# Keeping the low halves of split weights in DRAM between the two segments of a hybrid decoder block

## The chip, the cores and the metric

The kernel runs on one core of one Trainium2 chip. The metric is device time in microseconds. A core has TensorE (PE: matmuls, with PEld for its weight loads), VectorE (DVE), ScalarE (ACT), GpSimd (POOL) and SyncE (SP, which here only issues DMAs). Each engine works through its own instruction queue in order; DMAs are issued from the queues of SyncE, ScalarE or GpSimd and are moved by 16 DMA engines.

## The reference

The block takes 1024 tokens of width 1024, puts 16 meta tokens ahead of them, and applies a half-step SwiGLU, a mixer, a second half-step SwiGLU and a final norm, all in float32:

```python
h = h + 0.5 * _swiglu(_rmsnorm(h, ffn1_norm[l]), ffn1_w_gu[l], ffn1_w_down[l])
u = _rmsnorm(h, mix_norm[l])
aq, ak, av, az, abeta, aalpha, bcols, ga, gb = jnp.split(u @ w_in[l], ...)
o_a = _deltanet_branch(...)      # chunked gated DeltaNet, 8 heads of 128
o_b = _rwkv7_branch(...)         # RWKV-7 time mixing, 16 heads of 64
merged = jax.nn.sigmoid(ga) * o_a + jax.nn.sigmoid(gb) * o_b
h = h + merged @ w_out[l]
h = h + 0.5 * _swiglu(_rmsnorm(h, ffn2_norm[l]), ffn2_w_gu[l], ffn2_w_down[l])
```

The change touches the product `u @ w_in` alone, and of that only how its weights come to the chip.

## The kernel before

**Precision.** TensorE multiplies numbers of a shortened float32 format (F32R). To keep float32 accuracy each operand is split into a high part, the value rounded to F32R, and a low part, the rest. `split` (L159) does this with two instructions: ScalarE copies the source into the high part (L163), and VectorE subtracts that from the source for the low part (L164). `mm3` (L309) then adds three products for each of the eight slices of 128 rows: high weight with high data, high weight with low data, low weight with high data. So the low half of a weight tile is first wanted by the third product.

**Weights.** `w_in` is stored as 75 tiles `in_win[ct]` of 128 x 8 x 128 (512 KB each, 4 KB in a partition). `fetchw` (L251) loads one of them with a DMA of SyncE (L268) into a raw buffer `wraw` (two of these), then splits it into a buffer `w` of shape [128, 2, 8, 128] (two, `WB`): index 0 of the second axis is the high half, 1 the low half. `loadw` (L279) is called when a projection begins; it fetches up to one tile ahead of the one in use (`AHEAD`), so the tile after the current one is written into the buffer that the previous projection has just left.

**Two segments.** The 1040 columns of the mixer (16 meta tokens and 1024 tokens) are done in two segments: the first has the meta tokens and 512 tokens, the second the other 512. In each segment the 8 head groups j are gone through, so there are 16 steps, `it` = 0 to 15, and each weight tile is loaded and split twice, once in each segment. `USES` (L168) names the tiles of a step: 48+j, 40+j, 32+j in `new_b` (value, key and receptance of the RWKV part), 8+j, j, 16+j in `new_a` (key, query and value of the DeltaNet part) and 24+j, 59+j, 67+j in `gates`. Tiles 56 to 58 belong to `segment`, which works once for each segment. In the first segment a projection of `new_b` and `new_a` has 528 columns, in two parts; in the second all have 512, with 24 matmuls.

**Order.** The actions of a step are listed by hand in strings such as

```python
REGULAR = "merge_blocks transitions operands+ inverses+ chains gates finish decay++ new_b++ new_a++"
```

where a `+` means one step ahead, so several steps are in flight. The framework traces the program in this order and then plans the order of each engine's queue itself; it also puts in all waits. So instructions of several actions stand mixed in one queue. In one step of the second segment, `chains` runs the recurrences over chunks while projections fill the gaps (products p, pq, b); `inverses` is a long row of small VectorE instructions (tb at L1657, Xb at L1659) ending in a copy (Yt, L1660) that goes out by DMA; `new_b` turns the three projections into rB, kB, kkn, AR, BK and bv, and `bon` is a product of the split of bv; `merge_blocks` and `transitions` make products xp, vp, mp and np, with ScalarE copies (xa, at, xv) between.

**GpSimd's queue in the mixers** has small work: zeroing the first columns of `sh` and `xr`, saving the last columns of a segment (carB, carA), the memsets of the inverses (Xb), copies of XA, egl, gam, and the start state SBs of the chain. DMAs from its queue occur once before the mixers' steps (rdr) and around the output projection (h2dr, h3dr); ScalarE's queue issues DMAs only at the kernel's beginning and end.

Of the kernel before, what the change touches and what calls it, by code (L numbers as in the profile page):

```python
# [8 lines left out]
F32 = mybir.dt.float32  # L9
F32R = mybir.dt.float32r  # L10
AF = mybir.ActivationFunctionType
ALU = mybir.AluOpType

P = 128
D = 1024
KD = D // P
# [21 lines left out]
NJ = 8  # L38
# [72 lines left out]
def build(tc, nc, a):  # L111

    ctx = ExitStack()
    with ctx:
        g = K()
        g.tc, g.nc, g.a = tc, nc, a
        nc.scalar.preload_act_table_set("natural_log_exp_and_others")
        pad = ctx.enter_context(tc.tile_pool(name="pad", bufs=1, side="right"))
        nc.vector.memset(pad.tile([P, 24], F32, name="pad"), 0.0)
        const = ctx.enter_context(tc.tile_pool(name="const", bufs=1))  # L120
        wp = ctx.enter_context(tc.tile_pool(name="wp", bufs=2))
        dram = ctx.enter_context(tc.tile_pool(name="dram", bufs=1, space=bass.MemoryType.DRAM))
        g.mmctx = ctx.enter_context(ExitStack())
        main_banks(g, 2, 3, 8)
        g.const, g.wp, g.dram = const, wp, dram

        ones = const.tile([P, P], F32, name="ones")
        nc.vector.memset(ones, 1.0)
        g.pk = const.tile([P, NPK], F32, name="pk")
        nc.sync.dma_start(g.pk, a["pk"])  # L130

        def pv(n):
            o, w = PK[n]
            return g.pk[:, o : o + w]

        nc.vector.tensor_scalar(pv("omu"), pv("mu"), -1.0, 1.0, op0=ALU.mult, op1=ALU.add)
        nc.vector.tensor_scalar(pv("oka"), pv("ka"), -1.0, 1.0, op0=ALU.mult, op1=ALU.add)
        for n in ("w0", "a0"):
            nc.vector.tensor_scalar(pv(n), pv(n), -1.0, None, op0=ALU.mult)
        g.C = lambda n: ones if n == "ones" else g.ck[:, CK[n][0] - P : CK[n][0] - P + CK[n][1]]  # L140
        g.V = lambda n, i=0: g.pk[:, PK[n][0] + i : PK[n][0] + i + 1]

        hdr = [dram.tile([KD, P, sn], F32, name=f"hdr{s}") for s, (_, sn, _) in enumerate(SEGS)]
        mdr = [dram.tile([NJ, P, FULL], F32, name=f"mdr{s}") for s in range(2)]
        g.hdr, g.mdr = hdr, mdr
        g.sdr = dram.tile([NJ, P, P + CB], F32, name="sdr")
        g.gdr = [dram.tile([NJ, FULL], F32, name=f"gdr{s}") for s in range(2)]
        g.rdr = dram.tile([P, FULL], F32, name="rdr")
        g.h2dr = dram.tile([KD, P, FULL], F32, name="h2dr")
        g.h3dr = dram.tile([KD, P, FULL], F32, name="h3dr")  # L150
        g.frm = dram.tile([len(FORMS), HF, P, T // 2], F32, name="frm")

        g.worder, g.wready, g.wfetched, g.wused = list(weight_order()), [], 0, 0
        ffn1(g)
        middle(g)
        ffn2(g)


def split(g, src, hi, lo, eng=None, hi_eng=None):  # L159
    if hi_eng:  # L160
        hi_eng.tensor_copy(hi, src)
    else:
        g.nc.scalar.activation(hi, src, AF.Copy)  # L163
    (eng or g.nc.vector).tensor_tensor(lo, src, hi.bitcast(F32), op=ALU.subtract)  # L164


LORA = (56, 57, 58)
USES = {"segment": LORA, "new_b": (48, 40, 32), "new_a": (8, 0, 16), "gates": (24, 59, 67)}  # L168


def schedule():

    last = 2 * NJ - 1
    yield "segment", 0
    for act in FIRST.split():
        yield act.rstrip("+"), act.count("+")
    for it in range(last + 1):
        order = {NJ - 2: BEFORE_SWITCH, NJ - 1: SWITCH, last - 1: LAST_BUT_ONE, last: FINAL}.get(it, REGULAR)
        for act in order.split():
            if act == "segment":  # L180
                yield act, 1
            else:
                yield act.rstrip("+"), it + act.count("+")
# [11 lines left out]
def weight_order():  # L195

    def down_order(n):
        for r in range(len(FORMS)):
            for m in range(HK):
                for k0, kk in CHUNKS:  # L200
                    yield f"wdn{n}", (r, m, k0), kk

    def tiles(cts, j=0):
        for ct in cts:
            yield "win", (ct + j % NJ,), KD

    yield from down_order(1)
    for act, it in schedule():
        yield from tiles(USES.get(act, ()), 0 if act == "segment" else it)
    for _ in range(2):  # L210
        for m in range(KD):
            yield "wout", (m,), KD

    yield None
    yield from down_order(2)
# [14 lines left out]
def down_weights(g, name, raw, r, m, k0, kk, copied):  # L230

    s = g.wsum[:, m, k0 : k0 + kk]
    if r == 4 and k0 == 0:
        in_turn(g, g.wsum[:, m], block(g, name, m, 0, 0))
    if raw is None:
        return s
    i, j = ((1, 0), (0, 0), (0, 1), None, (1, 0), (0, 1))[r - 1]
    in_turn(g, raw, g.wlast[m, :, k0 : k0 + kk] if copied else block(g, name, m, i, j, k0, kk))
    if r == LAST:
        return raw  # L240
    x, y = (raw, s) if r == 3 else (s, raw)
    g.nc.gpsimd.tensor_tensor(s, x, y, op=ALU.add if r == 1 else ALU.subtract)  # L242
    return s


def held(g, what):

    return what[0].startswith("wdn") and what[1][0] == LAST and len(g.held) > 0


def fetchw(g):  # L251
    if not g.worder[g.wfetched]:
        del g.worder[g.wfetched]
    name, idx, kk = g.worder[g.wfetched]
    g.wfetched += 1
    down = name.startswith("wdn")
    raw = w = None
    if held(g, g.worder[g.wfetched - 1]):
        w = g.held.pop(0)
        raw = w[:, 1, :kk].bitcast(F32)  # L260
    elif not down or idx[0] not in (0, 4):
        raw = g.wp.tile([P, KD, P], F32, name="wraw", tag="wraw", bufs=2)[:, :kk]
    if down:
        src = down_weights(g, name, raw, *idx, kk, w is not None)
        g.wcount += 1
    else:
        src = raw
        g.nc.sync.dma_start(raw, g.a[name][idx])  # L268
    if w is not None:
        pass  # L270
    elif down and g.wcount % 3 == 0:
        w = g.wthird.tile([P, 2, CHUNKS[0][1], P], F32R, name="w3", tag="w3", bufs=1)
    else:
        w = g.wp.tile([P, 2, KD, P], F32R, name="w", tag="w", bufs=WB)
    split(g, src, w[:, 0, :kk, :], w[:, 1, :kk, :])
    g.wready.append((name, idx, w))


def loadw(g, name, *idx):  # L279

    while g.wfetched < len(g.worder) and g.worder[g.wfetched]:
        down = g.worder[g.wfetched][0].startswith("wdn")
        if g.wfetched > g.wused + AHEAD + down and not held(g, g.worder[g.wfetched]) or (name == "wdn1" and not down):
            break
        fetchw(g)
    g.wused += 1
    n, i, w = g.wready.pop(0)
    assert (n, i) == (name, idx)
    return w


def main_banks(g, w, n, banks=6):

    g.mmctx.close()
    g.mmw = w
    pool = lambda name, bufs: g.mmctx.enter_context(
        g.tc.tile_pool(name=name, bufs=bufs, space=bass.MemoryType.PSUM, reuse_waits="tile"))
    g.mm = pool("mm", n)
    g.mx = pool("mx", banks - n * w)
# [356 lines left out]
class Hidden:  # L656
# [16 lines left out]
    def ahead(self):  # L673
        g = self.g
        g.wcount, g.turn, g.held, g.direct = 0, None, [], self.direct
        sums = lambda m: g.nc.sync.dma_start(g.wsum[:, m], block(g, self.name, m, 1, 1))
        self.even += self.places("11", "21")
        self.slots = self.even[:]
        self.load(8, 0)
        yield  # L680
        yield
        sums(0)
        fetchw(g)
        self.split(3)
        yield
        self.even += self.places("t2")
        self.slots = self.even[:HF]
        self.load(HF, 0)
        self.split(6)
        yield  # L690
        sums(1)
        self.split(8)
        yield
        fetchw(g)
        self.split(HF - 1)
        for m in (2, 3):
            sums(m)
        yield
# [1296 lines left out]
```

## Time and profile before

| what | value |
|---|---|
| median of 3 runs | 2974.12 us (2969.96 to 2985.99) |
| profiled execution | 2974.08 us, span 2972.3 us |
| busy share, PE / DVE / ACT / POOL | 97% / 74% / 49% / 17% |
| L164 low parts from `wraw`, whole kernel | 254, 338.2 us |
| L163 high parts from `wraw`, whole kernel | 254, 266.9 us |
| `wraw<-in_win` | 150 DMAs of 512 KB, SyncE's queue |
| GpSimd's DMA queue | 2000 packets, 6.56 MB |
| ScalarE's DMA queue | 2016 packets, 2.63 MB |

The two SwiGLUs take the time up to about 700 us and from about 2300 us on; the mixers lie between, their first segment up to about 1480 us. In the page's list of instruction groups one line such as L164 gathers every use of `split`, with its mean over different shapes, so times of one use are better read from the row of a single instruction. A row of the timeline gives start, length, engine, line, operation and tiles, and in brackets how long the engine stood idle before it and what released it.

### The profile page before, as it was taken

The page shows a single profiled execution, that of the slowest core. Times are in us where ns is not written, and L with a number is a line of the kernel's source. Part 1 is how long each engine was busy: PE and PEld are TensorE (multiplying, and loading weights), DVE is VectorE, ACT ScalarE, POOL GpSimd, SP SyncE. Part 2 cuts the span into 40 slices and gives each one's busy share as a digit, 9 for nine tenths or more (in the row PEclk, how much of TensorE's full clock was granted, in tenths as well). Part 3 has the DMA queues.
Part 4 walks back from the last instruction along what each step waited for, and adds up shares of the span by engine and source line. Part 5 has one row for each costly group of instructions (what it writes and reads, how often), then busy time and mean ns, then how long its engine had stood idle before and what let it go on. Part 6 is the DMA issues. An engine that isn't in the chain of part 4 may idle for free.

```text
span 2972.3 us, 63124 instructions
## 1 busy us (share of the span) xinstructions
PE 2876.8 (97%) x25720; PEld 2496.4 (84%) x25720; DVE 2208.8 (74%) x4121; ACT 1450.5 (49%) x2559; POOL 503.4 (17%) x578
## 2 busy tenths in 40 slices
PE   8999999999899999999998999999999999999998
PEld 8999999999878888888776777777777888888887
DVE  8666668776667877788878887778876766667886
ACT  6322234346555656565566556556644422223443
POOL 0332232323000000000000000001101032332431
PEclk9999999999999999999999999999999999999999
DMA  5333236553232322333232332333345332333763
GB/s 212 125 108 108 98 124 206 182 193 118 71 70 72 86 65 68 84 81 85 89 98 73 80 79 77 76 87 82 106 132 185 127 109 99 97 102 130 248 220 113
DMA packets 287907, 339.39 MB, mean 114 GB/s; under 512 B 172704, under 2 KB 181024, under 8 KB 287616
## 3 DMA queue, kind: packets, MB, share of 16 engines
q1 hardware_dynamic: 283600, 326.17, 36.0%
q0 software_dynamic: 2000, 6.56, 0.6%
q8 instruction: 202, 3.31, 0.5%
q10 hardware_dynamic: 2016, 2.63, 0.2%
q14 instruction: 89, 0.73, 0.1%
HBM read 267.63 MB, written 73.41 MB: 115 GB/s over the span
## 4 chain that ended last, share of the span: by engine, by line
PE 67%; DVE 19%; ACT 6%; issue 3%; DMA 3%; SPq 1%; POOL 0%; DVEq 0%; ACTq 0%; POOLq 0%
PE pg L521 25%; PE pp L315 15%; PE pd L742 10%; DVE w L164 3%; PE pwo L315 2%; PE pg L545 2%; DVE tb L1657 1%; DVE Xb L1659 1%; DVE form L164 1%; ACT w L163 1%; PE vp L1342 1%; DMA form<-frm 1%; PE mp L1342 1%; PE xp L1342 1%; PE np L1342 1%
## 5 line engine op out<-in xcount | busy, mean ns | idle before, releaser
L315 PE MATMUL pp<-uk,w 128*128 128x512 f32 (+2 forms) x4824 | 971.3, 347 | 13.8 <-DVE w L164 5.9
L315 PEld LDWEIGHTS pp<-uk,w 128*128 128x128 f32 x4824 | 745.4, 191 | 111.7 <-DVE w L164 14.7
L742 PE MATMUL pd<-form,w 128*128 128x256 f32 (+2 forms) x2904 | 437.3, 312 | 5.4 <-DVE w L164 5.2
L742 PEld LDWEIGHTS pd<-form,w 128*128 128x128 f32 x2904 | 402.7, 189 | 39.5 <-DVE w L164 7.3
L521 PE MATMUL pg<-bt,w 128*128 128x256 f32 (+2 forms) x2520 | 401.9, 318 | 3.1 <-DVE w L164 2.5
L521 PEld LDWEIGHTS pg<-bt,w 128*128 128x128 f32 x2520 | 360.2, 188 | 37.3 <-DVE w L164 3.8
L527 DVE TENSOR_TENSOR c<-c,pg 128x520 f32<-128x520 f32 (+1 forms) x280 | 189.4, 688 | 239.1 <-PE pg L521 215.8
L164 DVE TENSOR_TENSOR w<-wraw,w 128x1024 fp32r<-128x1024 f32 (+1 forms) x254 | 338.2, 1332 | 38.7 <-ACT w L163 37.1
L521 PE MATMUL pg<-b,w 128*128 128x256 f32 (+2 forms) x2160 | 348.1, 317 | 0.0
L163 ACT ACTIVATE w<-wraw 128x1024 fp32r<-128x1024 f32 (+1 forms) x254 | 266.9, 1052 | 164.1 <-PE pg L521 117.4
L521 PEld LDWEIGHTS pg<-b,w 128*128 128x128 f32 x2160 | 309.9, 188 | 28.3 <-DVE w L164 0.3
L163 ACT ACTIVATE w<-wrx 128x1024 fp32r<-128x1024 f32 (+1 forms) x64 | 58.4, 912 | 279.0 <-PE pg L521 239.2
L491 POOL TENSOR_TENSOR wrx<-wrx 128x512 f32<-128x512 f32 x38 | 52.5, 1381 | 612.8 <-DVE w22b L164 351.6
L164 DVE TENSOR_TENSOR form<-form 128x520 fp32r<-128x520 f32 (+1 forms) x152 | 145.8, 995 | 14.0 <-ACT form L163 13.8
L163 ACT ACTIVATE w<-wsum 128x768 fp32r<-128x768 f32 x96 | 75.6, 788 | 155.8 <-PE pd L742 117.1
L164 DVE TENSOR_TENSOR w<-wsum,w 128x768 fp32r<-128x768 f32 x96 | 112.9, 1181 | 37.3 <-ACT w L163 37.3
L163 ACT ACTIVATE form<-form 128x520 fp32r<-128x520 f32 (+1 forms) x152 | 93.8, 631 | 79.5 <-DMA form<-frm 73.4
L242 POOL TENSOR_TENSOR wsum<-wsum,wraw 128x768 f32<-128x768 f32 (+1 forms) x48 | 97.6, 2050 | 204.7 <-DMA wraw<-in_wdn 154.3
L1659 DVE TENSOR_TENSOR Xb<-Xb,tb 115x126 f32<-115x126 f32 (+22 forms) x496 | 125.2, 252 | 8.7
L1657 DVE TENSOR_TENSOR tb<-Ub,Xb 115x126 f32<-115x126 f32 (+22 forms) x496 | 124.5, 251 | 9.5 <-DMA Ub<-scr 2.0
L1466 DVE SCALAR_TENSOR_TENSOR acc<-xr,pk,acc 128x528 f32<-128x528 f32 (+1 forms) x144 | 109.0, 757 | 20.6 <-ACT acc L1462 19.9
L315 PE MATMUL pwo<-uk,w 128*128 128x512 f32 x384 | 95.3, 397 | 1.3 <-DVE uk L164 0.6
(439 smaller groups left out, 4421.4 us busy)
## 6 DMA issues: line engine op xcount, KB each, us to landing
wraw<-in_win SPq DMA_DIRECT2D x150, 512.0 KB
wraw<-in_wgu SPq DMA_DIRECT2D x44, 512.0 KB
wrx<-in_wgu SPq DMA_DIRECT2D x44, 512.0 KB
frm<-c SPq DMA_DIRECT2D x76, 260.0 KB
form<-frm SPq DMA_DIRECT2D x76, 260.0 KB
frm<-c SPq DMA_DIRECT2D x76, 256.0 KB
form<-frm SPq DMA_DIRECT2D x76, 256.0 KB
wraw<-in_wdn SPq DMA_DIRECT2D x34, 384.0 KB
```

The costliest lines, as they stand in the source:

```text
L163: g.nc.scalar.activation(hi, src, AF.Copy)
L164: (eng or g.nc.vector).tensor_tensor(lo, src, hi.bitcast(F32), op=ALU.subtract)
L242: g.nc.gpsimd.tensor_tensor(s, x, y, op=ALU.add if r == 1 else ALU.subtract)
L315: g.last_product = g.nc.tensor.matmul(ps, lhsT=l, rhs=r, start=i == 0, stop=i == n - 1)
L521: nc.tensor.matmul(ps[:, c0 : c0 + cn], lhsT=l[:, x, k, :], rhs=r[:, k, y, c0 : c0 + cn], start=i == 0, stop=i == 3 * HK - 1)
L527: nc.vector.tensor_tensor(o, x, y, op=ALU.add)
L545: nc.tensor.matmul(ps[:, c0 : c0 + cn], lhsT=l[:, x, k, :], rhs=r[:, k, y, c0 : c0 + cn], start=i == 0, stop=i == 6 * HK - 1)
L742: nc.tensor.matmul(pd[:, c0 : c0 + cn], lhsT=wd[:, u, k - k0, :], rhs=x[:, v, c0 : c0 + cn], start=k + i == 0, stop=k == HF - 1 and i == 2)
L1342: g.nc.tensor.matmul(ps[e][HS[dst], c0 : c0 + CB], lhsT=l, rhs=r, start=True, stop=True)
L1466: nc.vector.scalar_tensor_tensor(acc[:, :n], xr[:, tap : tap + n], V("convw", ct * 4 + tap), acc[:, :n], op0=ALU.mult, op1=ALU.add)
L1657: nc.vector.tensor_tensor(tv, U[:, i, i + 1 :].unsqueeze(2).to_broadcast([npt, nt, ncc]), X[:, i, 0:ncc].unsqueeze(1).to_broadcast([npt, n ...
L1659: nc.vector.tensor_tensor(X[:, i + 1 :, 0:ncc], X[:, i + 1 :, 0:ncc], tv, op=ALU.add)
```

## The change

A DRAM tensor `wlow` gets one place for each of the 75 tiles. `KEPT` lists 45 tiles: 41 to 47, 33 to 39, 9 to 15, 24 to 31, 59 to 66 and 67 to 74, which are six of a step's nine (three of them not for j = 0). When such a tile is first fetched, in the first segment, it is split as before and its low half is stored to `wlow` by a DMA from GpSimd's queue. When it is fetched again, in the second segment, the low half is read from `wlow` into the weight buffer by a DMA from ScalarE's queue, and ScalarE's copy makes the high half from the raw tile as before; there is no subtraction. The raw tile is loaded both times.

```diff
+        g.wlow = dram.tile([75, P, KD, P], F32, name="wlow")
+        g.lows = set()
...
+KEPT = [ct + j for ct, j0 in ((40, 1), (32, 1), (8, 1), (24, 0), (59, 0), (67, 0)) for j in range(j0, NJ)]
...
-    split(g, src, w[:, 0, :kk, :], w[:, 1, :kk, :])
+    low = w[:, 1, :kk, :]
+    if name == "win" and idx[0] in g.lows:
+        g.nc.scalar.dma_start(low.bitcast(F32), g.wlow[idx[0]])
+        g.nc.scalar.activation(w[:, 0], src, AF.Copy)
+    else:
+        split(g, src, w[:, 0, :kk, :], low)
+        if name == "win" and idx[0] in KEPT:
+            g.nc.gpsimd.dma_start(g.wlow[idx[0]], low.bitcast(F32))
+            g.lows.add(idx[0])
```

## The prediction

> **What bounds the kernel now.** I read the stage table first, then the waits of TensorE in the second segment, then one step of that segment engine by engine. The columns of the table are the stretch, its length, busy us (instructions) of TensorE, its weight loads, VectorE, ScalarE and GpSimd, the granted clock, the DMA share and GB/s.
>
> ```profile
> span 2972.3 us, 63124 instructions
> ...
> 736.00:1480.00 744.00, 711.11 (x8392) 609.50 (x8391) 565.37 (x1399) 432.58 (x877) 46.98 (x163) 0.98 0.30 78
> 1480.00:2205.00 725.00, 694.56 (x7620) 552.71 (x7619) 578.65 (x1358) 444.71 (x842) 57.92 (x124) 0.99 0.32 84
> 1784.00:1871.00 87.00, 84.20 (x943) 66.97 (x942) 70.54 (x167) 52.92 (x103) 8.09 (x15) 1.00 0.31 83
> 1844.00:1850.00 6.00, 6.00 (x28) 4.88 (x26) 5.93 (x14) 4.82 (x10) 2.30 (x1) 1.00 0.00 0
> 2280.00:2292.00 12.00, 10.34 (x42) 7.31 (x41) 8.04 (x12) 8.26 (x14) 1.09 (x2) 1.00 0.83 324
> ```
>
> The first two rows are the mixers' first and second segment; the third is one regular step of the second. VectorE is busy 70.5 of a step's 87 us, so six subtractions fewer look like a lot. But TensorE is busy 84.2 of 87, and it is in-order: time can be won only where TensorE stands still for want of VectorE. A busy TensorE need not be at its peak, so its rate has to be looked at too.
>
> ```profile
> 1850.83 5.94 PE L315 MATMUL pp<-uk,w 128*128 128x512 f32 x24
> ...
> 1857.08 8.80 PE L315 MATMUL pp<-uk,w 128*128 128x512 f32 x38
> 1867.39 0.50 PE L1289 MATMUL bon<-hl,bdr 128*128 128x512 f32 x1 [1.52 <-ACT hl L163]
> ```
>
> ```profile
> PE bon L1289 <- ACT hl L163: 1.5, 1, 1.5
> PE xp L1342 <- ACT at L1753: 0.5, 1, 0.5
> PE np L1342 <- DVE AR L1768: 0.4, 1, 0.4
> ...
> PE pp L315 <- DVE w L164: 4.2, 2, 2.8
> PE pp L315 <- ACT acc L1462: 3.0, 1, 3.0
> PE bon L1289 <- ACT hl L163: 1.6, 2, 1.1
> ```
>
> The 38 products take 0.232 us each, and the 24 of one projection 0.248: the stretch in which the chain of waits runs through VectorE is, for TensorE, a stretch at nearly full rate, with one hole of 1.5 us before bon. The first three wait rows are of 1790 to 1880 us, a regular step; the last three of 1600 to 1700 us, the first two steps on the new segment, where VectorE is further behind. So there are 1.5 us per regular step, and 8.8 us once, that a lighter VectorE can touch at all.
>
> **The change part by part.** Per step nine tiles of w_in are split; six are kept. KEPT has 3 x 7 + 3 x 8 = 45 tiles: 40, 32 and 8 for seven steps, 24, 59 and 67 for eight.
>
> *Removed: 45 subtractions in the second segment.* The rows of one step, with the ScalarE copy that comes before each:
>
> ```profile
> 1847.63 1.04 ACT L163 ACTIVATE w<-wraw 128x1024 fp32r<-128x1024 f32 x1
> ...
> 1850.90 1.05 ACT L163 ACTIVATE w<-wraw 128x1024 fp32r<-128x1024 f32 x1
> ...
> 1856.81 0.69 ACT L1202 ACTIVATE rB<-pp,pk 128x512 f32<-128x512 f32 x1 [3.10 <-PE pp L315]
> ```
>
> ```profile
> 1850.22 1.22 DVE L164 TENSOR_TENSOR w<-wraw,w 128x1024 fp32r<-128x1024 f32 x1
> ...
> 1852.77 1.22 DVE L164 TENSOR_TENSOR w<-wraw,w 128x1024 fp32r<-128x1024 f32 x1
> ...
> 1858.68 0.75 DVE L1203 SCALAR_TENSOR_TENSOR rB<-pp,pk,rB 128x512 f32<-128x512 f32 x1
> ...
> 1860.47 1.22 DVE L164 TENSOR_TENSOR w<-wraw,w 128x1024 fp32r<-128x1024 f32 x1
> 1861.61 0.75 DVE L1419 SCALAR_TENSOR_TENSOR kkn<-kB,pk,kkn 128x512 f32<-128x512 f32 x1
> ...
> 1865.93 0.75 DVE L1438 SCALAR_TENSOR_TENSOR bv<-rB,pk,kB 128x512 f32<-128x512 f32 x1
> ```
>
> A subtraction holds VectorE 1.14 us (1860.47 to the next start, 1861.61), so 51 us leave an engine that is busy 579 in this segment. Only two (tiles 32 and 8, at 1850.22 and 1852.77) and tile 40's a little before lie in the stretch that ends at bon. How much of it reaches bon? rB could have started when ScalarE ended, 1857.50; VectorE took it at 1858.68, 1.2 us late. From rB to bv lies VectorE work of 7.3 us that the change leaves alone, tile 0's subtraction among it. So of 3.4 us taken off, 1.2 us reach bon, perhaps the whole 1.5 as the final copy of the inverses is drawn ahead too. I take 1.2; ends 0 and 1.5. Five regular steps (11 to 15) give 6 us. In the two steps of 1600 to 1700 us the relief is at most 2 x 3 x 1.14 = 6.8 of the 8.8 us; I take 5, ends 0 and 6.8. Step 8 has only its gates kept, and no VectorE wait to lose. Together -11 us (0 to -14.3). What is late next is ScalarE and TensorE's own products.
>
> *Added to ScalarE: 45 DMA issues.* ScalarE issues DMAs at the kernel's end:
>
> ```profile
> L1043 ACTq DMA_DIRECT2D out_dram<-fin x12: 338/344/390, 2935.4 to 2968.1; - x12
> ```
>
> ```profile
> 1802.68 0.63 ACT L1212 ACTIVATE zg<-zg 128x512 f32<-128x512 f32 x1
> 1803.22 1.04 ACT L163 ACTIVATE w<-wraw 128x1024 fp32r<-128x1024 f32 x1
> 1804.17 0.62 ACT L1213 ACTIVATE zg<-zg 128x512 f32<-128x512 f32 x1
> 1804.81 0.66 ACT L1755 ACTIVATE xa<-xp 128x256 f32<-128x256 f32 x2
> ```
>
> 0.34 us each, 15.5 us in all, on an engine busy 445 of 725. The issue waits for what the copy behind it waited for, the weight buffer's release by TensorE, so it holds the ScalarE queue no longer than before. It costs where ScalarE is last: tile 67's copy at 1803.22 stands ahead of xa and at, for which TensorE waits 0.5 us. 8 steps x 0.34 = +2.7 us (0 if the issue falls into a hole, 5.5 if tile 40's issue counts too).
>
> *Added: the low part comes by DMA.* It must land before the third product of its tile. Landing times are shown for 512 KB twice in the chain, and for 256 KB on GpSimd's queue:
>
> ```profile
> 1.19 4.73 DMA wraw<-in_wgu
> ...
> 2369.49 5.43 DMA wraw<-in_wgu
> ```
>
> ```profile
> L946 POOL DMA_DIRECT2D h3dr<-hh x8: 539/540/544, 2280.1 to 2319.4; - x8
> ...
> DMA to landing us min/median/max: 2.3/2.6/8.4
> ```
>
> ```profile
> 1785.17 1.05 ACT L163 ACTIVATE w<-wraw 128x1024 fp32r<-128x1024 f32 x1
> ...
> 1791.61 1.55 PE L315 MATMUL pp<-uk,w 128*128 128x512 f32 x6
> ```
>
> Both 512 KB rows stand amid other loads. In 1844 to 1850 us the DMA engines are idle (share 0.00), so my estimate is the median of 256 KB, 2.6, plus another 256 KB at the 324 GB/s of the stage table, 0.8: 3.4 us; ends 2.3 and 5.43. Tile 32 is the tightest: issue at 1847.63, 0.34, 3.4: landed at 1851.4, against 1851.36 when the subtraction ended before (its product starts at 1850.83). No cost; with 4.73 it is 1.3 us late, with 5.43 2.1. The other five, with 5.43: tile 24 1785.17 + 0.34 + 5.43 = 1790.9, its third product at 1791.6; tile 8 1856.7, needed at 1857.5; tiles 40, 59 and 67 are fetched a whole projection or more ahead. Cost 0 (ends 0 and 2.1 x 7 = 14.7 us).
>
> [...] By the 4.73 us row instead, tile 32 is 1.3 us late in seven steps, and the sum is 9 us dearer, about +2.
>
> *Added to GpSimd and the DMA engines, first segment: 45 stores.* 0.54 us each by the h3dr row, 24 us on an engine busy 47 of 744, and 23.6 MB, which at 78 GB/s for a share of 0.30 lifts the share to about 0.42. A store waits for its subtraction; behind it in GpSimd's queue stand small copies that mostly wait longer themselves. The store can itself stand behind such a wait:
>
> ```profile
> 1170.81 1.22 DVE L164 TENSOR_TENSOR w<-wraw,w 128x1024 fp32r<-128x1024 f32 x1
> 1179.38 0.70 POOL L1386 COPY gam<-ELx 128x8 f32<-128x8 f32 x1 [22.48 <-ACT ELx L1384]
> 1189.87 1.05 ACT L163 ACTIVATE w<-wraw 128x1024 fp32r<-128x1024 f32 x1
> ```
>
> Tile 40's low part is ready at 1172.0; behind gam its store goes out by 1180.6 and lands, with the worst 8.4 us, at 1189.0, before the buffer is written again at 1189.87. That margin is the cover; without it ScalarE's copy, and one projection behind it, would wait. I put +1 us for the small transfers of the inverses meeting stores (0 to 5).
>
> *Raw loads.* In the second segment a raw buffer comes free after the copy instead of after the subtraction, so SyncE's loads of w_in start up to 3 us earlier. That wins nothing, since ScalarE hardly waits for them, and could only draw loads into each other.
>
> Sum: -11 + 2.7 + 0 + 1 = -7.3. The profiled execution took 2974.08 us (span 2972.3 and 1.8 around it), the median is 2974.12, so no correction: **2967 us**, inside the 0.5% (14.9 us) that can be told from no change.
>
> **The rivals.**
>
> *Late low parts (slower).* With 5.43 us nothing but tile 32 slips; at 6.9, halfway to the 8.4 of the h3dr row, tile 32 is 3.5 us late, tile 24 0.8; less the 1.5 us hole at bon that is 2.8 per step, x 7 + 3.7 = +23: 2997 us. It decides (over 2989) from a landing of about 6.3 us. For it: both 512 KB rows stand amid other loads, and six loads more per step (23.6 MB over 725 us, 33 GB/s on 84) raise the share from 0.32 by some 0.13. Against: the idle moment of tile 32. [...]
>
> *VectorE was the real bound (faster).* The 30.4 us that TensorE idles in 1480 to 2205 us are mostly waits on VectorE and ScalarE. If the lighter VectorE lets the planned order close up, two thirds may go: 2954 us. For it: VectorE is busy 5.93 of 6 us before bon. Against: xp, np and vp wait on short chains that no subtraction delays.
>
> *It doesn't pay.* The work behind rB still ends at bon, or ScalarE's extra 0.34 us takes what is won: 2974 us. The 270 VectorE and ScalarE instructions of a step (167 and 103 in the stage table) may also be laid out in another order, which the trace can't price; I allow 8 us of either sign, the size of the sum itself.
>
> *Stores hold weight buffers.* If stores land 2 us behind the 1189.87 us (the 8.4 us stand for half the bytes), the first segment loses 2 us in each of 8 steps, +16 on the sum: 2983 us.
>
> **How the numbers follow.** Forecast 0.45; doesn't pay 0.13; stores 0.05; late low parts 0.16; VectorE bound 0.21. The likeliest gives 2967, its own range 2959 to 2979. All but 2 in 10 lies within 2952 to 2991. Faster by over 0.5% (under 2959): 0.22, the VectorE case and an edge of the forecast; slower (over 2989): 0.17; between: 0.61.
>
> **What would show it.** VectorE's busy time in the second segment falls by about 51 us; the 1.5 us at bon is gone or under 0.4; regular steps go from 87 to about 86 us; ScalarE's queue shows 45 issues of about 0.34 us; the first segment's steps stay within 0.5 us of theirs. Wrong, if TensorE's products wait for a DMA into w (late low parts), if a step falls under 85 us, or if the first segment moves by more than 5 us.

## The result and the profile after

The changed kernel takes 2992.12 us (median of 8 runs, 2982.16 to 2999.34) against 2974.14 (8 runs, 2969.96 to 2985.99): a ratio of 1.0061, 95% interval 1.0048 to 1.0074. The forecast was 2967 with a range of 2952 to 2991, so the time went the other way and ended just above the range. Lines of the new kernel from the weight loading on stand 12 higher than those of before (L315 is L327, L1289 is L1301), the two of `split` 2 higher (L163 is L165); new are L281, ScalarE's load of a low part, L282, ScalarE's high copy of a kept tile, and L286, GpSimd's store. In the experiments e5, e8 and e9 some lines stand one higher still, in e1 one lower, and in e2 L281 is the copy and L282 the load.

First the span, the busy times of the engines from the page of after, and the stage table of after, with the columns of the prediction's table:

```profile
span 2989.7 us, 63279 instructions
...
PE 2882.0 (96%) x25720; PEld 2506.9 (84%) x25720; DVE 2167.5 (72%) x4076; ACT 1452.6 (49%) x2559; POOL 511.9 (17%) x623
```

```profile
736.00:1480.00 744.00, 708.48 (x8370) 607.02 (x8370) 561.40 (x1392) 428.76 (x870) 68.97 (x207) 0.98 0.39 107
1480.00:2205.00 725.00, 683.70 (x7552) 549.13 (x7551) 523.65 (x1285) 434.99 (x821) 42.53 (x124) 0.98 0.40 114
1940.00:1950.00 10.00, 9.56 (x63) 7.49 (x64) 6.11 (x19) 4.46 (x10) 0.05 (x1) 0.83 0.81 208
```

VectorE did become lighter: 523.65 us busy in the second segment instead of 578.65. Part of that difference is work that has moved out of the fixed window of 725 us; over the whole kernel VectorE is busy 2167.5 us instead of 2208.8, which is 41.3 less. TensorE did less in the same 725 us, 683.70 instead of 694.56. The third row shows ten microseconds in which TensorE is busy for 9.56 at a granted clock of 0.83; the last section comes back to such stretches. The waits of TensorE from 1480 to 2205 us, in us, times and longest, say what it stood for:

```profile
PE pp L327 <- ACT w L282: 16.9, 5, 3.4
PE vap L1490 <- DVE acc L1482: 8.4, 7, 2.4
...
PE pp L327 <- DMA w<-wlow: 1.5, 1, 1.5
PE bon L1301 <- ACT hl L165: 0.2, 1, 0.2
```

In before the row of bon in the same stretch is

```profile
PE bon L1289 <- ACT hl L163: 8.9, 7, 1.5
```

These 8.9 us are gone, as meant. In their place the products of a projection wait for *ScalarE's high copy*, once in each regular step, 3.39 us. The loaded low part is waited for once in the segment, for 1.5 us. Two timelines of one step of after show it, TensorE first, then ScalarE (ACTq rows are what its queue issues):

```profile
1936.19 0.85 PE L327 MATMUL pp<-uk,w 128*128 128x512 f32 x3
1940.43 7.37 PE L327 MATMUL pp<-uk,w 128*128 128x512 f32 x24 [3.39 <-ACT w L282]
```

```profile
1928.63 0.60 ACT L1223 ACTIVATE gg<-pp 128x512 f32<-128x512 f32 x1 [2.08 <-PE pp L327]
1928.69 0.33 ACTq L281 DMA_DIRECT2D w<-wlow  x1
1929.26 0.64 ACT L1224 ACTIVATE gg<-gg 128x512 f32<-128x512 f32 x1
...
1932.17 0.67 ACT L1382 ACTIVATE sw<-pw,pk 128x512 f32<-128x512 f32 x1
...
1938.82 0.61 ACT L1396 ACTIVATE ELx<-Ls 128x512 f32<-128x512 f32 x1
1939.34 1.04 ACT L282 ACTIVATE w<-wraw 128x1024 fp32r<-128x1024 f32 x1
1940.29 0.67 ACT L1214 ACTIVATE vB<-pp,pk 128x512 f32<-128x512 f32 x1
```

The same copy in before, in the same place of the step:

```profile
1923.88 0.60 ACT L1211 ACTIVATE gg<-pp 128x512 f32<-128x512 f32 x1 [1.21 <-PE pp L315]
1924.38 1.05 ACT L163 ACTIVATE w<-wraw 128x1024 fp32r<-128x1024 f32 x1
1925.33 0.62 ACT L1212 ACTIVATE gg<-gg 128x512 f32<-128x512 f32 x1
```

Before, the copy of tile 40's kind started 0.50 us behind gg. After, the *load* has that place and the copy starts 10.71 us behind gg. ScalarE stands idle for 1.6 of these microseconds; else it does the work of `finish` and `decay` first. Nothing made the copy wait: its place in the planned order of ScalarE's queue has changed, in every regular step in the same way.

Where the 17.4 us of span (2989.7 against 2972.3) come from can be read off the start of the first product grb of each step. The table gives for before and after the time from the first grb of step 0 to that of step 8 (the first segment), the next two steps, the mean of the five regular steps behind them, and the TensorE time lost to a granted clock under 1 from 1480 to 2205 us (busy time x (1 - clock), summed over windows of 2 us). The experiments of the next section stand in the same table; their ratio to before has its 95% interval. Each row's times are those of one execution, and executions of one kernel differ by some microseconds with the clock that they are granted (of the 29 of before beside e9 to e12 the shortest, 2962.67 us, has a mean clock of 0.996, the longest, 2988.94 us, one of 0.990; the profiled ones of e8 and e11 lie 11 and 8 us under their medians), so the ratios carry the comparison of whole times and the rows show where in a kernel the time lies.

| kernel | ratio | first segment | next two steps | regular step | clock loss |
|---|---|---|---|---|---|
| before | 1 | 768.5 | 169.1 | 87.0 | 2.8 |
| after | 1.0061 (1.0048 to 1.0074) | 773.3 | 157.8 | 91.8 | 10.9 |
| e1 stores only | 1.0015 (1.0003 to 1.0027) | 772.9 | 168.7 | 86.9 | 2.9 |
| e2 copy first | 1.0164 (1.0144 to 1.0184) | 773.4 | 175.0 | 95.5 | 34.2 |
| e3 load from SyncE | 0.9957 (0.9939 to 0.9974) | 775.5 | 160.8 | 86.0 | 1.5 |
| e4 load from GpSimd | 0.9966 (0.9953 to 0.9980) | 770.3 | 161.3 | 85.8 | 3.1 |
| e5 only 40 moved | 1.0062 (1.0048 to 1.0077) | 772.6 | 180.3 | 86.6 | 17.3 |
| e6 gates from 1 | 0.9979 (0.9969 to 0.9989) | 765.4 | 165.8 | 85.8 | 3.2 |
| e7 nine kinds | 1.0004 (0.9990 to 1.0017) | 777.4 | 158.6 | 87.1 | 1.7 |
| e8 VectorE's work kept | 1.0018 (1.0003 to 1.0033) | 772.2 | 166.8 | 86.6 | 3.1 |
| e9 only gates moved | 1.0062 (1.0040 to 1.0085) | 771.0 | 160.6 | 91.5 | 15.9 |
| e10 three kinds | 0.9977 (0.9963 to 0.9991) | 769.0 | 166.8 | 85.6 | 2.9 |
| e11 gates only | 1.0004 (0.9989 to 1.0019) | 769.0 | 163.3 | 87.1 | 4.5 |
| e12 SyncE, gates from 1 | 0.9978 (0.9965 to 0.9991) | 767.2 | 165.0 | 86.0 | 2.9 |

So the changed kernel gains 11.3 us in the two steps behind the switch to the second segment and loses 4.8 in the first segment and 23.9 in five regular steps, 17.4 in all.

### The profile page after: what moved, and what is told of

It is laid out like the page before. It is cut to its first block, busy times and chain, and to the rows that moved or that the text cites. A ratio compares the mean times of both kernels' runs of the same rounds, so it can differ in the third digit from the quotient of the medians.

```text
span 2989.7 us, 63279 instructions
## 1 busy us (share of the span) xinstructions
PE 2882.0 (96%) x25720; PEld 2506.9 (84%) x25720; DVE 2167.5 (72%) x4076; ACT 1452.6 (49%) x2559; POOL 511.9 (17%) x623
## 2 busy tenths in 40 slices
DMA packets 300867, 386.59 MB, mean 129 GB/s; under 512 B 174144, under 2 KB 182464, under 8 KB 300576
## 5 line engine op out<-in xcount | busy, mean ns | idle before, releaser
L327 PE MATMUL pp<-uk,w 128*128 128x512 f32 (+2 forms) x4824 | 975.7, 349 | 25.1 <-ACT w L282 16.9
L327 PEld LDWEIGHTS pp<-uk,w 128*128 128x128 f32 x4824 | 751.8, 192 | 125.0 <-ACT w L282 19.6
L166 DVE TENSOR_TENSOR w<-wraw,w 128x1024 fp32r<-128x1024 f32 (+1 forms) x209 | 281.6, 1348 | 39.1 <-ACT w L165 37.6
L165 ACT ACTIVATE w<-wraw 128x1024 fp32r<-128x1024 f32 (+1 forms) x209 | 219.8, 1052 | 155.6 <-PE pg L533 115.9
L165 ACT ACTIVATE w<-wrx 128x1024 fp32r<-128x1024 f32 (+1 forms) x64 | 58.4, 912 | 278.2 <-PE pg L533 239.4
L165 ACT ACTIVATE w<-wsum 128x768 fp32r<-128x768 f32 x96 | 75.7, 788 | 152.9 <-PE pd L754 123.4
L165 ACT ACTIVATE form<-form 128x520 fp32r<-128x520 f32 (+1 forms) x152 | 94.1, 632 | 81.5 <-DMA form<-frm 73.6
L1669 DVE TENSOR_TENSOR tb<-Ub,Xb 115x126 f32<-115x126 f32 (+22 forms) x496 | 124.3, 251 | 10.2 <-DMA Ub<-scr 1.2
L327 PE MATMUL pwo<-uk,w 128*128 128x512 f32 x384 | 94.9, 397 | 0.0
```

The lines of the kernel that those rows point to most:

```text
L327: g.last_product = g.nc.tensor.matmul(ps, lhsT=l, rhs=r, start=i == 0, stop=i == n - 1)
L1669: nc.vector.tensor_tensor(tv, U[:, i, i + 1 :].unsqueeze(2).to_broadcast([npt, nt, ncc]), X[:, i, 0:ncc].unsqueeze(1).to_broadcast([npt, n ...
```

## The experiments

My theory (A) was that the loss is the late high copy, brought about by two instructions of one queue where there had been one. Rivals: the traffic of the loads and stores or re-planned work of other engines (B), low parts that come late (C), the gate tiles' copies (D).

**e1: the stores alone.**

```diff
-    if name == "win" and idx[0] in g.lows: (load and copy)
-    else:
+    split(g, src, w[:, 0, :kk, :], low)        # every time; the store stays
```

> Only the 45 stores of the first segment remain; in the second segment every tile is split as before, and what is stored is never read. Theory A (the loss lies in the second segment, where ScalarE's copy of the high part comes late in its queue): first segment about 2.7 us longer as in the changed kernel, second as before, 2977 us (2974 to 2980). Rival B (the stores' traffic or the re-planned orders that they bring are the loss): 2985 to 2992 us.

Measured: 2978.22 us. The second segment is that of before (168.7 us, steps of 86.9), as A says. The stores and what they bring cost 1.0015, some 4 us, all in the first segment; the rest of the loss is in the second. One place of that cost is visible. In the first segment's waits the row of before is `PE iv L1692 <- DMA Xc<-scX: 1.7, 1, 1.7`, and in e1:

```profile
PE iv L1703 <- DMA Xc<-scX: 4.6, 1, 4.6
```

**e2: the same two instructions, the other way round.**

```diff
+        g.nc.scalar.activation(w[:, 0], src, AF.Copy)
         g.nc.scalar.dma_start(low.bitcast(F32), g.wlow[idx[0]])
-        g.nc.scalar.activation(w[:, 0], src, AF.Copy)
```

> The two writes of a kept tile change places in the program: ScalarE's high copy first, then the load of the low part, still from ScalarE's queue. In the planned order the high copy is back where it was before the change (right behind gg), and the load of tile 40's low part stands where the copy stood, some 11 us later, just ahead of vB. Theory A (the second of two instructions in one queue is put late, whichever it is): no PE wait on the high copy; instead waits of PE on the load w<-wlow of 1 to 5 us in each regular step (the load would be issued at about 1937, land 3.4 to 7 us later, and the third product of a tile begins about 5 us after its first), 2978 to 2995 us. Rival B (the late copy does not matter): 2992 us with the same PE stretch as the changed kernel. Rival C (the low part is in time even so): 2965 to 2975 us.

Measured: 3025.54 us, worse than all that I had allowed. The place in the queue came out as expected: the copy follows gg at once, the load has the late place. In ScalarE's timeline:

```profile
1953.12 0.58 ACT L1223 ACTIVATE gg<-pp 128x512 f32<-128x512 f32 x1
1953.59 1.05 ACT L281 ACTIVATE w<-wraw 128x1024 fp32r<-128x1024 f32 x1
...
1961.62 0.33 ACTq L282 DMA_DIRECT2D w<-wlow  x1
...
1962.05 0.38 ACTq L282 DMA_DIRECT2D w<-wlow  x1
```

How it hurt was not as expected. My text put the third product 5 us behind the first; in this kernel each slice has its three products in a row, so the low part is wanted some 0.5 us behind the start, as the prediction had it. And the waits are not on the load. TensorE's waits of 1480 to 2205 us are

```profile
PE vbp L1354 <- DVE vB L1215: 28.5, 6, 4.8
PE vap L1490 <- DVE acc L1482: 13.7, 7, 2.0
```

because in the planned order vbp now stands ahead of most of that projection's products, where before all 24 stood ahead of it, and TensorE waits for vB with the products behind it. So what costs the time in e2 is a changed order of TensorE, and that the late load brought that order about is argued, not shown. That the second of the two is put late, whichever it is, holds.

**e3 and e4: the load from another queue.**

```diff
-        g.nc.scalar.dma_start(low.bitcast(F32), g.wlow[idx[0]])
+        g.nc.sync.dma_start(low.bitcast(F32), g.wlow[idx[0]])      # e3
+        g.nc.gpsimd.dma_start(low.bitcast(F32), g.wlow[idx[0]])    # e4
```

> The low parts are loaded by SyncE's queue instead of ScalarE's; ScalarE's high copies stand in the planned order where they stood before the change. Theory A: the waits of PE on the high copy (16.9 us in five steps) go, regular steps return from 91-92 us to 86-87, 2967 to 2974 us (2.7 us of the first segment stay, what VectorE saves comes back). Rival B (the loads' traffic or the changed order of VectorE costs the time): 2985 to 2995 us. Rival C (SyncE's queue holds the loads behind raw tiles, so the low parts are late): waits of PE on w<-wlow, 2975 to 3000 us.

> The low parts are loaded by GpSimd's queue, where the stores stand too; ScalarE's queue has the high copies alone, where they stood before the change. Theory A: as with SyncE's queue, 2967 to 2974 us, if GpSimd's queue lets the loads go in time. Rival C (a load waits in GpSimd's queue behind memsets and copies, or holds those up while it waits for the buffer): PE waits on w<-wlow or on GpSimd's tiles, 2975 to 3000 us. Rival B: 2985 to 2995 us.

Measured: 2964.63 and 2965.69 us, both faster than before, 1 to 2 us under the range that A gave, and by the medians some 27 us under the changed kernel. ScalarE's timeline and TensorE's waits in e4:

```profile
1915.45 0.60 ACT L1223 ACTIVATE gg<-pp 128x512 f32<-128x512 f32 x1 [2.05 <-PE pp L327]
1915.94 1.05 ACT L282 ACTIVATE w<-wraw 128x1024 fp32r<-128x1024 f32 x1
```

```profile
PE xp L1354 <- ACT at L1765: 5.4, 7, 1.0
PE np L1354 <- DVE AR L1780: 3.9, 7, 0.6
...
PE bon L1301 <- ACT hl L165: 0.9, 2, 0.6
...
PE pp L327 <- DMA w<-wlow: 0.4, 1, 0.4
```

The copy is 0.49 us behind gg again, the waits on it are gone, bon waits 0.9 us instead of 8.9, regular steps take 85.8 us. Both kernels move as many bytes as the changed one (386.59 MB on the pages of after and of e4), so traffic (B) is not the loss, and the loads are not late (C): for e4 the profile gives the time from issue to landing, in minimum, median and maximum,

```profile
DMA to landing us min/median/max: 3.7/3.9/6.7
```

beside my estimate of 3.4 for the same 512 KB from ScalarE's queue, for which the profile of after gives none. The two kernels are the best that I ran; between them the intervals overlap.

**e5 and e9: which copy it is.** In e5 only the loads of tiles 41 to 47 go to GpSimd's queue, in e9 those of the gate tiles (24, 59 and 67 with their seven others each).

```diff
+        eng = g.nc.gpsimd if 40 <= idx[0] < 48 else g.nc.scalar                               # e5
+        eng = g.nc.scalar if 8 <= idx[0] < 48 and idx[0] // 8 != 3 else g.nc.gpsimd           # e9
+        eng.dma_start(low.bitcast(F32), g.wlow[idx[0]])
```

> As the changed kernel, but the low parts of tiles 41 to 47 are loaded by GpSimd's queue; those of the five other kinds stay with ScalarE's. In the planned order the high copies of 41 to 47 are back behind gg; the high copies of the gate tiles still stand 5 to 10 rows behind their load. Theory A (it is the late copy of tiles 41 to 47 that PE waits for, 3.4 us a step, with what follows it): the 16.9 us of waits on the high copy go, regular steps at 87 us or less, 2966 to 2975 us. Rival D (the gates' late copies and the 8.4 us of waits of vap on acc cost as much): waits on vap stay, 2979 to 2988 us.

> The complement of e5: the low parts of the gate tiles (24 to 31, 59 to 74) are loaded by GpSimd's queue, those of 33 to 39, 41 to 47 and 9 to 15 by ScalarE's. In the planned order the high copies of 41 to 47 stand 15 rows behind gg again. Theory A (each regular step loses 3.4 us to the late copy of tile 40's kind and about 1.8 us of lower granted clock right behind that hole): regular steps 90 to 92 us with one wait of 3.4 us each, 2985 to 2995 us. Rival D (the gates' copies on ScalarE are what matters): regular steps 86 to 87 us, 2965 to 2975 us.

Measured: 2989.85 and 2991.93 us. e9 went as A says: steps of 91.5 us, each with the 3.39 us wait. In its waits of 1480 to 2205 us that wait is whole, while the waits at vap, 7 in the changed kernel, are down to 2:

```profile
PE pp L328 <- ACT w L283: 16.9, 5, 3.4
PE vap L1491 <- DVE acc L1483: 2.6, 2, 2.4
```

In e5 the wait on the high copy of tile 40's kind is gone and the regular steps have lost most of their excess (82.7, 87.4, 88.7, 87.2 and 87.3 us, where the first holds 122 products fewer than the others and the last four are a little above the 87 that A allowed). But the time is as high as ever, above the range of A and, by 2 us, above that of D. The loss is now in one place, the steps from 1546.0 to 1726.3 us, of which the second is 104.3 us long. The holes in TensorE's timeline there, and the stage table over the same place:

```profile
1599.94 3.02 PE L328 MATMUL pp<-uk,w 128*128 128x512 f32 x6 [3.23 <-ACT acc L1475]
...
1618.68 0.50 PE L1302 MATMUL cs<-hl,onesr 128*128 128x512 f32 x1 [2.21 <-ACT hl L1316]
...
1676.95 7.36 PE L328 MATMUL pp<-uk,w 128*128 128x512 f32 x24 [1.96 <-ACT w L283]
```

```profile
1600.00:1640.00 40.00, 35.92 (x384) 27.21 (x386) 24.09 (x56) 21.90 (x42) 4.07 (x9) 0.71 0.44 106
1622.00:1726.30 104.30, 98.67 (x1166) 79.53 (x1166) 66.64 (x164) 56.88 (x111) 7.18 (x21) 0.91 0.35 100
```

TensorE waits little in the step from 1622.0 us, but the clock is 0.71 over 40 us, and the clock loss of the segment exceeds that of before by 14.5 us (17.3 against 2.8), about as much as the span does (2985.9 against 2972.3). That step also holds 1166 products of TensorE, where before had 988 in its own, so part of its length is work drawn ahead from the next. The three steps behind the switch together take 263.0 us in e5, 255.7 in before and 249.3 in the changed kernel.

What brings this loss about is open. Of the three holes the first is in before too (2.98 us), and only the last, 1.96 us, is a wait for the high copy of a kept tile. The loads of the gate tiles on ScalarE (D) can't be the cause alone: the changed kernel has them as well, and these steps are shorter there than in before. So e5 and e9 show which copy costs the regular steps their 3.39 us; that moving tile 40's loads alone would also save the time, they do not show. What saved it, in e3 and e4, was to take all the loads from ScalarE's queue.

**e6 and e12: the first segment's share.** The gate tiles of step 0 are left out (42 kept tiles), e6 with loads from GpSimd's queue, e12 from SyncE's.

```diff
-KEPT = [... (24, 0), (59, 0), (67, 0)) ...]
+KEPT = [... (24, 1), (59, 1), (67, 1)) ...]
```

> Loads of the low parts by GpSimd's queue, as in e4, and tiles 24, 59 and 67 (the gates of step 0) are left out of the kept ones, 42 instead of 45: their three stores stand where the first inverses' result goes out to DRAM and back, and there the first segment lost its time (PE waited 4.8 instead of 1.7 us for Xc<-scX). Theory F (these three stores hold up that transfer): the wait returns to 1.7 us and the time is 2.5 to 3 us under e4, 2961 to 2965 us. Rival G (the loss comes with the first stores, whichever they are): as e4, 2965 to 2968 us.

> The candidate for the best version: loads of the low parts by SyncE's queue, as in e3, and the gate tiles of step 0 not kept, as in e6. If the two add: the wait for Xc<-scX at 1.7 us, regular steps at 86 us, 2960 to 2965 us. If the gates of step 0 do not matter: as e3, 2963 to 2967 us.

Measured: 2967.42 and 2969.10 us; e6 is in the range of G and e12 above both of its ranges. The wait for Xc<-scX is back at 1.7 us in both, so it is these three stores that meet the first inverses' transfer, as F says; the first segment of both profiles is shorter than that of before. Yet the gain of 2.5 us is not in the medians: the ratios, 0.9979 and 0.9978, are no better than those of e4 and e3. The table shows where it goes: the first segment is 5 and 8 us shorter than in e4 and e3, the next two steps are 4.5 and 4.2 us longer (165.8 against 161.3, 165.0 against 160.8). The rows of e6, the first from the first segment, the second from 1480 to 2205 us:

```profile
PE iv L1704 <- DMA Xc<-scX: 1.7, 1, 1.7
PE pp L327 <- DVE w L166: 3.1, 2, 2.8
```

The second wait, 2.8 us for a subtraction in step 8, is that of before (`PE pp L315 <- DVE w L164: 4.2, 2, 2.8`). In e3 and e4, which keep the gate tiles of step 0 and so need not split them again in step 8, 0.3 us of this row are left. The same three tiles cost time in the first segment and save it in the second.

**e8, e10, e11, e7: what VectorE's relief is worth.** All load from GpSimd's queue.

```diff
+        g.nc.vector.tensor_tensor(src, src, w[:, 0, :kk, :].bitcast(F32), op=ALU.subtract)   # e8
-KEPT = [... ((40, 1), (32, 1), (8, 1), (24, 0), (59, 0), (67, 0)) ...]
+KEPT = [... ((40, 1), (32, 1), (8, 1)) ...]                                                  # e10
+KEPT = [... ((24, 0), (59, 0), (67, 0)) ...]                                                 # e11
+KEPT = [... ((48, 1), (0, 1), (16, 1), (40, 1), (32, 1), (8, 1), (24, 0), (59, 0), (67, 0)) ...]   # e7
```

> Loads of the low parts by GpSimd's queue, as in e4, but VectorE does the 45 subtractions all the same, into the raw tile, where nobody reads the result. Theory H (the gain of e4 is VectorE's time in the second segment): the waits of bon come back (about 9 us) and the time returns to 2975 to 2981 us, where e1 stands. Rival I (the gain is that the low part no longer waits for the copy and the subtraction behind it): 2964 to 2969 us as e4.

> Loads of the low parts by GpSimd's queue, as in e4, but only the tiles 33 to 39, 41 to 47 and 9 to 15 are kept (21). The prediction's account (only these three subtractions lie ahead of bon, and what they give is 1.2 us in a regular step): regular steps 85.5 to 86 us, the waits of bon nearly gone, 2965 to 2971 us. Rival J (the gates' subtractions count as well): regular steps 86.3 to 87 us, 2970 to 2976 us.

> Loads of the low parts by GpSimd's queue, as in e4, but only the 24 gate tiles are kept. The prediction's account: nothing is taken from the stretch that ends at bon, its waits of 1.5 us stay, regular steps 86.7 to 87.2 us, 2973 to 2979 us (the first segment still loses up to 3 us). Rival J (the gates' subtractions count): regular steps under 86.3 us, 2965 to 2972 us.

> Loads of the low parts by GpSimd's queue, as in e4, and all nine kinds of tiles of a step are kept (66 tiles instead of 45), so VectorE loses 21 more subtractions of about 1.2 us in the second segment. If VectorE is still what PE waits for there: 2955 to 2962 us. If the gain is spent once bon no longer waits (theory A): 2963 to 2969 us; late low parts of the 21 tiles or three more stores a step in the first segment could cost 1 to 5 us on top.

Measured: e8 2978.81, e10 2967.23, e11 2977.01, e7 2975.11 us. With VectorE's work put back (e8) the waits at bon are back and, by the ratio of 1.0018 against 0.9966, the gain is gone (H); the low part's shorter way is worth next to nothing by itself:

```profile
PE bon L1302 <- ACT hl L165: 7.1, 6, 1.5
```

With the three kinds alone that lie ahead of bon (e10), the regular step is 85.6 us, as short as with six, and the next two steps are 166.8 instead of 161.3: the gates' subtractions count behind the switch, where the 2.8 us wait of step 8 stays in e10 too, and not in a regular step. e11 is not settled. Its four last steps are 85.8, 87.1, 86.4 and 85.4 us and bon waits 1.0 us in all, less than I had said, but one step takes 91.0 with a hole of 1.94 us and 2.9 us of clock loss, and the median shows no gain. In e7 the three further kinds bring nothing: the first segment is longer by 7 us than in e4 (six waits on Xc<-scX, 8.2 us), and bon waits 7.1 us again in the order that this kernel got; its 2975.11 us lie above what I had allowed for either case.

## Why the prediction was wrong, by its steps

*What bounds it, and the relief.* Right in a regular step, and too small behind the switch. Where the copies stayed in place, six kinds kept gave 1.1 us per regular step (e1 86.9, e4 85.8; 1.2 said) and 7.4 in the two steps behind the switch (168.7 to 161.3; 5 said, end at 6.8). Together that is some 12.8 us, 11 said. e8 shows that it is VectorE's time. Behind the switch the prediction had the wrong tiles: it says that step 8 has "no VectorE wait to lose", but the 2.8 us wait that it had counted for the three other kinds stands in step 8 and goes only where the gate tiles of that step are kept (0.3 us left in e3 and e4, 2.8 in e6, e10 and e12).

*The low part comes in time.* Right: one wait of 1.5 us on w<-wlow in the changed kernel. The tight tile, 32, did not decide; rival "late low parts" did not occur.

*The stores.* Mis-sized: +1 (0 to 5) said, a ratio of 1.0015 measured in e1, which is 4.5 us (0.9 to 8.0). The meeting with the inverses' transfers was the right mechanism, and the wait for Xc<-scX grew at the stores of step 0 alone. No store held a weight buffer.

*45 issues from ScalarE: +2.7.* This step failed. It says that the issue "waits for what the copy behind it waited for" and so "holds the ScalarE queue no longer than before". The issue does take 0.33 us, and it goes out when the buffer comes free (at 1928.69, behind products that end at 1928.6). But the copy is not behind it: the planner gave the load the place that the copy had had and put the copy 15 instructions and 10.2 us later. In a regular step that is 3.39 us of waiting for tile 40's copy, 1.93 us of lower clock behind it (mean of the five, 1.65 to 2.85), and 1.00 us at vap, which goes where the gates' loads leave ScalarE (e9: 2 waits there instead of 7), less the 1.5 us at bon: +4.8, as measured (91.8 against 87.0). That the wait at vap costs the step its whole 1.00 us is not shown, since e9's steps are as long without it. I had costed a moved instruction by its duration and let the order of the queue stand. Among the rivals I did write that the order could change, "8 us of either sign"; the whole distance from e4 to the changed kernel is 26 us.

*The cover that the prediction named.* For tile 40 the prediction says that it is "fetched a whole projection or more ahead". That was so for the load; the product needs both halves, and the copy used up the projection.

*What would show it.* VectorE's busy time fell by 55.0 us in the window that the prediction named and by 41.3 over the whole kernel (51 said); bon fell to 0.2 us, and there are 45 issues of 0.33. Regular steps went to 91 to 92 us instead of 86, a sign of failure that I had not listed.

Why the planner puts the second of two instructions late was not tried directly. ScalarE has a gap ahead of gg in which one younger instruction finds room, and older work fills the queue behind it; e2 fits that, but it is argued, not shown.

## What to carry to other kernels

An added DMA issue is cheap by its time, 0.33 us here, and can be dear by its place: where a planner orders the queues, issue it from a queue for whose other work nobody waits at that moment (here SyncE's or GpSimd's), and look at where the neighbours of the new instruction went before summing durations. A hole in TensorE's work can cost more than its length: in the changed kernel the five of 3.39 us had 1.93 us of clock loss behind them on average, 5.3 us together, while those of 1.32 to 1.52 us in before had none. When a change loses time although its waits look small, compare the granted clock over short stretches before looking for more waits.

## What the runs showed of the hardware

I had not expected how often a dip of the granted clock stands right behind a hole. Two rows of stretches right behind a hole in before: 1.52 us ahead of bon at 1867.39, and 2.98, 1.06 and 2.82 us at 1600 to 1608.

```profile
1866.00:1876.00 10.00, 8.61 (x45) 6.77 (x47) 9.05 (x13) 5.26 (x10) 2.45 (x3) 1.00 0.42 115
1600.00:1612.00 12.00, 7.24 (x17) 4.64 (x18) 12.00 (x29) 5.64 (x9) 0.93 (x2) 0.57 0.15 44
```

In the second segments of before and after, seven holes of 1.32 to 1.52 us have no clock loss from 4 us before to 12 us behind them (0.0 each). At the two of 2.98 and 2.82 us in before the clock is at 0.50 for 10.24 us on end; behind the six of 2.38 to 3.39 us in after it is at 0.50 too, five times for 3.41 us and once, behind the last, for 6.83. In e9 the first of the five holes of 3.4 us has no dip behind it, the four others have one. And in e5, where TensorE is idle for 1.00 us from 2070 to 2072 and for 0.31 in the next two, a dip of 3.4 us begins at 2073.4, so the length of a hole does not decide alone.

The clock records show more. In before and after each record is at 1.00 or 0.50, and no window of 2 us from 1470 to 2210 us has less than 0.50 in any of the 14 profiles. In these windows there are 44 stretches at 0.50, 18 of them 3.41 us long, 18 of 6.83, 7 of 10.24 and one of 13.65 (to the 0.04 us that the windows resolve), and within a profile they begin whole multiples of 3.413 us apart. The stage table of e9, cut at these multiples into sections, shows what TensorE did in each of them, the first three rows at the hole without a dip, the last two at the same hole one step later (columns as in the prediction's table, the clock third from the end):

```profile
1752.13:1755.54 3.41, 1.74 (x7) 0.86 (x5) 3.24 (x9) 1.83 (x4) 0.00 (x0) 1.00 0.00 0
1755.54:1758.96 3.42, 1.70 (x7) 1.43 (x8) 3.35 (x10) 3.42 (x7) 0.54 (x1) 1.00 0.63 189
1758.96:1762.37 3.41, 3.41 (x16) 2.81 (x15) 3.18 (x13) 0.17 (x1) 0.00 (x0) 1.00 0.94 311
...
1844.29:1847.70 3.41, 1.01 (x4) 0.86 (x5) 3.27 (x10) 3.41 (x6) 0.55 (x1) 1.00 0.55 163
1847.70:1851.12 3.42, 3.42 (x9) 2.65 (x8) 3.22 (x14) 0.85 (x3) 0.00 (x0) 0.50 0.84 262
```

The first hole is shared by two sections, with 1.67 and 1.71 us idle, and no dip follows. The second leaves 2.40 us of one section idle, and in the next section the clock is 0.50. In the second segments of before and after, cut in the same way, seven sections at full clock have 1.97 to 3.28 us idle, and each is followed by one at 0.50; 407 have 1.50 us or less, and none of them is. That the hole makes the dip is read from this order in time; no run put in a hole by itself.
